# Entry of a two-layer diffusion backbone: the first two modulations' rows loaded two blocks per run into the activation places of two chunks

## The chip, the cores and the metric

The kernel runs as one program on one NeuronCore of a Trainium2 chip. The metric is the device time of one execution in microseconds (us), median over the runs; lower is better. All times below are from a profiled execution or from the timed runs of the kernel before the change.

## What is computed

The reference is a small diffusion backbone: 1024 latent tokens and 256 context tokens of width 1024, two layers. The first layer (even) mixes with four mLSTM heads beside 32 S5 state-space groups, the second (odd) with a gated DeltaNet; each layer also has a SwiGLU feed-forward part. What matters here stands at the very start. Every sub-layer normalises its rows and modulates them with a shift and a scale that come from a conditioning vector:

```python
s_lat = jax.nn.silu(c)
s_ctx = jax.nn.silu(c_ctx)
m_l = jnp.split((s_lat @ ada_w[i] + ada_b[i])[:, None, :], 6, axis=-1)
m_c = jnp.split((s_ctx @ ada_w[i] + ada_b[i])[None, None, :], 6, axis=-1)
hl = modulate(rmsnorm(x, norm1_w[i]), m_l[0], m_l[1])
hc = modulate(rmsnorm(ctx, norm1_w[i]), m_c[0], m_c[1])
```

`ada_w[i]` is 1024 x 6144 in float32; one modulation (shift or scale) needs a 1024 x 1024 block of it, 4 MB. Before the first projection of layer 0 can run, modulations 0 and 1 of layer 0 must be there, 8 MB of weights for two matrix-vector products each.

## The kernel before

Tokens are cut into three chunks: chunk 0 is the context (256 tokens), chunks 1 and 2 are 512 latent tokens each. A chunk is held transposed (features on the partitions) as `x0`, `x1`, `x2`. The normalised and modulated activations of a chunk are a pair of tiles `hh`/`hl` (a high and a low part, 128 x 8 x tokens, float32 bytes), allocated by `acts`; products run in three passes, high by high, low by high and high by low.

The function `entry` (line 1131) is the start of the program:

- `load_x` (line 329) loads the input in ten row blocks of 128 tokens x 1024 (512 KB each): two of the context, then eight latent ones, called x-block 0 to 7 below. Each lands in a tile `x_raw` of pool `araw`. ScalarE squares it and sums over the row (line 344; the squares themselves go to `junk`, a part of an activation tile), TensorE transposes it in eight pieces (line 349), VectorE and ScalarE copy the pieces into `x0` to `x2` (lines 352 and 354).
- `cond_steps` (line 182) makes one modulation. It loads `ada_w` in runs of `kk` row blocks (line 191), multiplies each block with the conditioning vector `svec` (line 194), copies the sum out of PSUM (`a_sb`, line 198), transposes it (`a_pt`, line 202) and adds the bias (`mod`, line 206); for the scale it also makes `amod` (line 210).
- `s5_poles` computes the poles of the S5 groups on VectorE, a chain of some 120 small instructions (lines 785 to 890); it needs only its own small inputs.
- `norm` makes the reciprocal root of a chunk's row sums (lines 223 and 94 to 102, VectorE) and a diagonal matrix of it (`ntmp`, line 231); TensorE spreads it over the partitions (`nb_ps`, line 275). `norm_part` then makes the eight feature blocks of `hh` and `hl` (lines 287, 289, 281 on VectorE, ScalarE, VectorE).
- `u_in` (S5 inputs) are the first projections of layer 0: they need `hh`/`hl` and the weights `w_raw` (line 113), which ScalarE rounds to `w_hi` (line 117) and GpSimd subtracts to `w_lo` (line 118).

Before the change `cond_many([(0, 0), (0, 1)], 1)` loads one row block (512 KB) per run, 16 runs. The tiles `a_raw` and `x_raw` share one tag of pool `araw` with three buffers, so a run of `ada_w` waits until the run or the x-block three loads earlier has been used. Every DMA of this stage is issued by SyncE (SP) in one order; a transfer also waits until the transfer eight issues earlier is complete, because the issues take eight semaphores in turn.

TensorE's instructions run in the order of the program text in this stage; on VectorE, ScalarE and SP the order is set by the framework's scheduler.

Of the kernel before, what the change touches and what calls it, by code (L numbers as in the profile page):

```python
# [6 lines left out]
F32 = mybir.dt.float32  # L7
# [9 lines left out]
P = 128  # L17
D = 1024
# [24 lines left out]
class Kernel:  # L43
# [135 lines left out]
        self.hnw = self.const.tile([P, 4], F32, name="hnw")  # L179
        nc.vector.tensor_scalar(out=self.hnw, in0=self.ncols[:, 32:36], scalar1=0.5, scalar2=None, op0=ALU.mult)  # L180

    def cond_steps(self, i, m, kk):


        nc = self.nc
        w = self.ins["ada_w"][i]
        ps = self.psm.tile([P, 512], F32, name="a_ps", tag="pm")
        for k0 in range(0, KB, kk):
            raw = self.araw.tile([P, kk, D], F32, name="a_raw", tag="a_raw")
            src = w[k0 * P:(k0 + kk) * P, m * D:(m + 1) * D]  # L190
            self.last_load = nc.sync.dma_start(out=raw, in_=src.rearrange("(k p) n -> p k n", p=P)).ins
            for k in range(k0, k0 + kk):
                for j in range(4):
                    nc.tensor.matmul(ps[32 * j:32 * j + 32, :256], self.svec[:, k], raw[:, k - k0, j * 256:(j + 1) * 256],
                                     start=(k == 0), stop=(k == KB - 1), tile_position=(0, 32 * j))
            yield
        sb = self.small.tile([P, 256], F32, name="a_sb", bufs=1)
        nc.vector.tensor_copy(sb, ps[:, :256])
        yield
        pt = self.psm.tile([P, 512], F32, name="a_pt", tag="pm")  # L200
        for h in range(2):
            nc.tensor.transpose(pt[:, h * P:(h + 1) * P], sb[:, h * P:(h + 1) * P], self.ident)
        src = pt[:, :256].rearrange("p (h j r) -> p j h r", h=2, r=32)[:, :, :, 0:2]
        dst = self.mod[:, i, m * 8:(m + 1) * 8].rearrange("p (j h) v -> p j h v", h=2)
        bias = self.adab[:, i, m * 8:(m + 1) * 8].rearrange("p (j h) -> p j h", h=2).unsqueeze(3)
        nc.vector.tensor_tensor(out=dst, in0=src, in1=bias.to_broadcast([P, 4, 2, 2]), op=ALU.add)
        if m in (1, 4):
            s = m // 4
            nw = self.ncols[:, 16 * s + 8 * i:16 * s + 8 * i + 8].unsqueeze(2).to_broadcast([P, 8, 2])
            nc.vector.scalar_tensor_tensor(out=self.amod[:, i, s], in0=self.mod[:, i, m * 8:(m + 1) * 8], scalar=1.0,  # L210
                                           in1=nw, op0=ALU.add, op1=ALU.mult)
        yield

    def cond_many(self, units, kk):
        for i, m in units:
            yield from self.cond_steps(i, m, kk)


    def norm_rstd(self, ssum_cols, n, scale=1.0 / D):
# [109 lines left out]
    def load_x(self, hs):  # L329

        nc = self.nc
        self.x = []
        self.ssq = self.const.tile([P, NCH], F32, name="ssq0")
        junk = hs[2][1].rearrange("p k t -> p (k t)")[:, :D]
        for ci, (t0, n) in enumerate(CHUNKS):
            xt = self.xp.tile([P, KB, n], F32, name=f"x{ci}")
            self.x.append(xt)
            src = self.ins["ctx"][0] if ci == 0 else self.ins["x"][0]
            r0 = 0 if ci == 0 else t0 - NCTX
            for j in range(n // P):  # L340
                raw = self.araw.tile([P, D], F32, name="x_raw", tag="a_raw")
                self.last_load = nc.sync.dma_start(out=raw, in_=src[r0 + j * P:r0 + (j + 1) * P, :]).ins
                ti = t0 // P + j
                nc.scalar.activation(out=junk, in_=raw, func=AF.Square, accum_out=self.ssq[:, ti:ti + 1])
                for h in range(2):
                    pt = self.psd.tile([P, 512], F32, name="x_pt", tag="pd")
                    for b in range(4):
                        f = h * 4 + b
                        nc.tensor.transpose(pt[:, b * P:(b + 1) * P], raw[:, f * P:(f + 1) * P], self.ident)
                    o = xt[:, h * 4:h * 4 + 4, j * P:(j + 1) * P]  # L350
                    if h == 0:
                        nc.vector.tensor_copy(o, pt.rearrange("p (b t) -> p b t", b=4))
                    else:
                        nc.scalar.copy(out=o, in_=pt.rearrange("p (b t) -> p b t", b=4))
                yield
# [372 lines left out]
    def emit(self, *streams):  # L728

        for _ in self.merge(streams):  # L730
            pass
# [399 lines left out]
    def entry(self, hs, mp, keep, st):  # L1131


        nc = self.nc
        norms = []

        def norm(ci):
            t0, n = CHUNKS[ci]
            rstd = self.norm_rstd(self.ssq[:, t0 // P:(t0 + n) // P], n // P)
            norms.append(self.norm_part(0, 0, ci, 0, n, hs[ci], rstd))  # L1140
            emit(norms[ci], 2)

        def emit(gen, n=1000):
            for _ in self.take(gen, n):
                pass

        x = self.load_x(hs)
        with ExitStack() as s1:
            cp = self.pool("cp", 1, st=s1)
            self.cond_vectors(cp)  # L1150
            poles = self.s5_poles(keep)
            next(poles)
            emit(x, 2)
            cond = self.cond_many([(0, 0), (0, 1)], 1)
            emit(cond, 2)
            emit(poles)
            emit(cond, 2)
            self.cond_columns(cp)
            emit(self.merge([(cond, 16), (self.take(x, 4), 4)]))
        u_in = self.s5_inputs(hs, mp, self.pool("wu", 1, st=st))  # L1160
        with self.tc.issue_after(self.last_load):
            emit(u_in, 1)
        norm(0)
        norm(1)
        emit(norms[0])
        emit(x, 2)
        emit(u_in, 3)
        emit(x)
        emit(norms[1])
        norm(2)  # L1170
        emit(u_in, 3)
        emit(norms[2])
        emit(u_in, 3)
        with self.tc.issue_after(self.last_load):
            for ci, (t0, n) in enumerate(CHUNKS):
                nc.sync.dma_start(out=self.x_dr[:, :, t0:t0 + n].rearrange("k p t -> p k t"), in_=self.x[ci])
        return u_in
# [214 lines left out]
    def layer0(self):  # L1392
# [6 lines left out]
        with ExitStack() as s0:  # L1399
            sk = ExitStack()  # L1400
            self.hy = self.hy2 = self.pool("hp", 1, st=s0)
            mp = self.pool("mp", 2, st=s0)
            gr = self.pool("mgr", 1, st=s0)
            self.s5k = self.pool("s5q", 1, st=sk)
            hs = [self.acts(ci) for ci in range(3)]
            with ExitStack() as s1:
                self.xp = self.pool("xp", 1, st=s1)
                self.araw = self.pool("araw", 3, st=s1)
                self.ntmp = self.pool("ntmp", 2, st=s1)
                order = ExitStack()  # L1410
                order.enter_context(self.in_pe_order())
                u_in = self.entry(hs, mp, mg, s1)
            self.even_select(mg)
            proj = self.mlstm_project(hs, mp)
            rows = self.mlstm_gate_rows(hs, gr)
            s5p = self.pool("s5s", 1, st=s5, other=True), self.pool("s5t", 2, st=s5, other=True)
            work = self.chain(u_in, rows, self.take(proj, NI))
            self.emit((self.take(work, W1), W1), (self.s5_inputs_outputs(), 5))
            self.emit((self.take(work, W2), W2))
            self.emit((work, 6 + NI - W1 - W2), (self.s5_in_matrices(), 16))  # L1420
            self.emit((self.take(proj, NJ), NJ))
            self.emit((self.take(proj, NP), NP), (self.s5_states(*s5p), 16))
            self.emit((self.take(proj, NK), NK))
            self.emit((self.take(proj, NQ), NQ), (self.s5_out_matrices(), 8))
            sk.close()
            self.emit((self.take(proj, NR), NR), (self.mlstm_gates(mg), 9))
            self.conv_taps()
            self.araw = self.pool("araw", 2, st=s0)
            self.emit((proj, 48 - NI - NJ - NK - NP - NQ - NR), (self.cond_many([(0, m) for m in range(2, 6)], 2), 24))
# [30 lines left out]
        places = ([wr.tile([P, KB * P], F32R, name=f"w_{p}") for p in ("hi", "lo")] for _ in range(KB // 2))  # L1460
# [939 lines left out]
```

## Time and profile before

| | |
|---|---|
| median of 3 timed runs | 3572.6 us (3568.52 to 3575.85) |
| the profiled execution's own time | 3570.8 us |
| its span, first to last instruction | 3568.8 us |
| mean granted TensorE clock | 0.967 |
| TensorE busy | 3341.3 us (94%) |
| VectorE busy | 1863.7 us (52%) |
| ScalarE busy | 1006.6 us (28%) |
| GpSimd busy | 971.9 us (27%) |

The page cuts the span in 40 slices of 89 us. In the first slice TensorE is busy for 5 tenths, its granted clock is 0.6 and the DMA engines are busy for 7 tenths; from the fourth slice on TensorE is nearly always at 9 or more. A busy TensorE is not one at its peak, since the ends of matmuls are modelled; idle time of an engine that nothing waits for costs nothing.

### The profile page before, as it was taken

To read this page: it belongs to the slowest core of one execution; us is meant where nothing else is said; L and a number is where in the kernel's file an instruction comes from. 1 tells how busy PE (TensorE), PEld (TensorE's weight loads), DVE (VectorE), ACT (ScalarE), POOL (GpSimd) and SP (SyncE) were. 2 spreads that over 40 slices of the span, in tenths; PEclk is the share of its full clock that TensorE was granted. 3 is DMA by queue.
4 is the path that set the end of the run, shared out by engine and by line. 5 is a ranking of instruction groups with operands and counts; after the bars stand their busy time and mean duration, and the time that the engine had idled before them with its cause. 6 is when DMAs were issued, how large, how long until landed. Compare 5 with 4: busy or idle time off the path is not lost. (4 is left out here: it accounts for less than half of the span.)

```text
span 3568.8 us, 48262 instructions
## 1 busy us (share of the span) xinstructions
PE 3341.3 (94%) x18518; PEld 2796.5 (78%) x18527; DVE 1863.7 (52%) x4024; ACT 1006.6 (28%) x2409; POOL 971.9 (27%) x843
## 2 busy tenths in 40 slices
PE   5998979899999999999988999888999999999999
PEld 3787768788888888888777877668897788888888
DVE  6749977624433333333467777776654432323234
ACT  3221125422111111111245545543444211111112
POOL 1011123241111111111342382753334122222223
PEclk6999989999999999999999999899999999999999
DMA  7454676331222121121123334356553011111111
GB/s 235 112 172 128 211 197 192 107 127 36 77 83 66 60 83 60 59 71 42 54 69 97 117 119 125 119 139 204 170 167 111 18 54 45 53 45 54 42 53 65
DMA packets 396187, 360.29 MB, mean 101 GB/s; under 512 B 104123, under 2 KB 329115, under 8 KB 395446
## 3 DMA queue, kind: packets, MB, share of 16 engines
q1 hardware_dynamic: 395958, 357.22, 32.4%
q8 instruction: 146, 2.39, 0.3%
q14 instruction: 83, 0.68, 0.1%
HBM read 258.92 MB, written 96.75 MB: 100 GB/s over the span
## 5 line engine op out<-in xcount | busy, mean ns | idle before, releaser
L124 PE MATMUL pd<-hh,w_hi 128*128 128x512 f32 (+1 forms) x3064 | 1158.2, 378 | 3.0 <-ACT hh L289 2.0
L126 PE MATMUL pd<-hh,w_lo 128*128 128x512 f32 (+1 forms) x3064 | 1134.6, 371 | 5.6 <-POOL w_lo L118 5.2
L125 PE MATMUL pd<-hl,w_hi 128*128 128x512 f32 (+1 forms) x3064 | 1137.5, 371 | 2.4 <-DVE hl L281 2.2
L118 POOL TENSOR_TENSOR w_lo<-w_raw,w_hi 128x1024 fp32r<-128x1024 f32 (+2 forms) x205 | 479.8, 2341 | 2001.5 <-ACT w_hi L117 1977.3
L124 PEld LDWEIGHTS pd<-hh,w_hi 128*128 128x128 f32 x3064 | 587.1, 192 | 118.4 <-issue 6.0
L126 PEld LDWEIGHTS pd<-hh,w_lo 128*128 128x128 f32 x3064 | 585.8, 191 | 111.4 <-POOL w_lo L118 9.3
L125 PEld LDWEIGHTS pd<-hl,w_hi 128*128 128x128 f32 x3064 | 586.8, 192 | 102.4 <-DVE hl L281 5.3
L117 ACT CAST w_hi<-w_raw 128x1024 fp32r<-128x1024 f32 (+2 forms) x205 | 207.4, 1012 | 927.1 <-PE pd L125 695.2
L1344 DVE SCALAR_TENSOR_TENSOR x<-pd,mod,x 128x512 f32<-128x512 f32 (+1 forms) x408 | 265.6, 669 | 226.1 <-PE pd L126 226.1
L124 PE MATMUL pd<-g_hi,w_hi 128*128 128x512 f32 (+1 forms) x844 | 307.8, 365 | 0.0
L125 PE MATMUL pd<-g_lo,w_hi 128*128 128x512 f32 (+1 forms) x844 | 306.9, 364 | 0.0
L126 PE MATMUL pd<-g_hi,w_lo 128*128 128x512 f32 (+1 forms) x844 | 304.1, 363 | 0.6 <-POOL w_lo L118 0.6
L1703 DVE SCALAR_TENSOR_TENSOR cv_acc<-img,wcv,cv_acc 128x512 f32<-128x512 f32 x384 | 279.6, 751 | 40.0 <-ACT img L1674 24.9
L1332 DVE TENSOR_TENSOR ntmp<-ntmp,pd 128x512 f32<-128x512 f32 (+1 forms) x110 | 69.8, 634 | 416.0 <-PE pd L126 415.6
L1331 DVE SCALAR_TENSOR_TENSOR ntmp<-ntmp,pd 128x512 f32<-128x512 f32 (+1 forms) x110 | 69.7, 634 | 380.8 <-ACT ntmp L1330 380.8
L124 PEld LDWEIGHTS pd<-g_hi,w_hi 128*128 128x128 f32 x844 | 159.2, 189 | 27.9 <-ACT w_hi L117 2.5
L126 PEld LDWEIGHTS pd<-g_hi,w_lo 128*128 128x128 f32 x844 | 158.9, 188 | 26.4 <-POOL w_lo L118 1.0
L125 PEld LDWEIGHTS pd<-g_lo,w_hi 128*128 128x128 f32 x844 | 159.2, 189 | 24.5
L1334 DVE SCALAR_TENSOR_TENSOR g_lo<-ntmp,g_hi 128x512 fp32r<-128x512 f32 (+1 forms) x110 | 139.8, 1270 | 64.1 <-ACT g_hi L1333 64.1
L1333 ACT ACTIVATE g_hi<-ntmp 128x512 fp32r<-128x512 f32 (+1 forms) x110 | 64.7, 588 | 349.2 <-DVE ntmp L1332 348.9
L1330 ACT ACTIVATE ntmp<-pd 128x512 f32<-128x512 f32 (+1 forms) x110 | 60.7, 552 | 247.9 <-PE pd L126 247.9
L250 POOL TENSOR_TENSOR nacc<-nacc,ntmp 128x256 f32<-128x256 f32 (+1 forms) x72 | 74.2, 1035 | 125.5 <-ACT ntmp L246 124.0
(544 smaller groups left out, 4531.4 us busy)
## 6 DMA issues: line engine op xcount, KB each, us to landing
w_raw<-in_ffn_w_dram SPq DMA_DIRECT2D x106, 512.0 KB
a_raw<-in_ada_w_dram SPq DMA_DIRECT2D x40, 1024.0 KB
w_raw<-in_od_w_in_dram SPq DMA_DIRECT2D x32, 512.0 KB
w_raw<-in_ffn_w_dram SPq DMA_DIRECT2D x32, 384.0 KB
w_raw<-in_ev_w_in_dram SPq DMA_DIRECT2D x20, 512.0 KB
a_raw<-in_ada_w_dram SPq DMA_DIRECT2D x16, 512.0 KB
x_dr<-x SPq DMA_DIRECT2D x4, 2048.0 KB
p_dr<-mp_t SPq DMA_DIRECT2D x32, 256.0 KB
```

The lines of the kernel that those rows point to most:

```text
L117: nc.scalar.copy(out=hi, in_=raw)
L118: self.w_lo_engine.tensor_tensor(out=lo, in0=raw, in1=hi.bitcast(F32), op=ALU.subtract)
L124: mm(ps, lh, rh, start=first, stop=False)
L125: mm(ps, lh, rl, start=False, stop=False)
L126: mm(ps, ll, rh, start=False, stop=last)
L250: nc.gpsimd.tensor_tensor(out=acc, in0=acc, in1=sq, op=ALU.add)
L1331: nc.vector.scalar_tensor_tensor(out=th[:, :n], in0=th[:, :n], scalar=1.0, in1=p1, op0=ALU.add, op1=ALU.mult)
L1332: nc.vector.tensor_tensor(out=th[:, :n], in0=th[:, :n], in1=p3, op=ALU.mult)
L1333: nc.scalar.activation(out=gh[:, t0:t0 + n], in_=th[:, :n], func=AF.Copy, scale=0.5)
L1334: nc.vector.scalar_tensor_tensor(out=gl[:, t0:t0 + n], in0=th[:, :n], scalar=0.5, in1=gh[:, t0:t0 + n].bitcast(F32), op0=ALU.mult, op1=ALU ...
L1344: nc.vector.scalar_tensor_tensor(out=xd, in0=ps, scalar=g, in1=xd, op0=ALU.mult, op1=ALU.add)
L1703: nc.vector.scalar_tensor_tensor(out=a, in0=src, scalar=wc(i), in1=a, op0=ALU.mult, op1=ALU.add)
```

## The change

- `cond_steps` and `cond_many` take an iterator `places`. With it a run of `ada_w` lands in a place given from outside, not in a buffer of `araw`.
- `entry` allocates the activation pairs of chunks 1 and 2 (`hh1`, `hl1`, `hh2`, `hl2`, each 16 KB on a partition), cuts each in two, and loads all eight runs of two row blocks (1 MB each) there. Nothing waits for a buffer among these loads. They are called run 0 to 7 below.
- `araw` keeps its three buffers, now for the input blocks alone.
- The interleaving is written anew: run 0, the poles, `cond_columns`, then five steps of the modulations (runs 1 to 3, the copy and the transpose of modulation 0), then runs of modulation 1 with x-blocks 0 to 3 between.
- `hs` holds only chunk 0 at first; the pairs of chunks 1 and 2 are allocated a second time, in the same places, after the modulations. `junk` moves from chunk 2's `hl` to chunk 0's for the context and chunk 1, since chunk 2's holds weights by then.

```diff
-    def cond_steps(self, i, m, kk):
+    def cond_steps(self, i, m, kk, places=None):
...
-            raw = self.araw.tile([P, kk, D], F32, name="a_raw", tag="a_raw")
+            raw = next(places) if places else self.araw.tile([P, kk, D], F32, name="a_raw", tag="a_raw")
...
-        junk = hs[2][1].rearrange("p k t -> p (k t)")[:, :D]
         for ci, (t0, n) in enumerate(CHUNKS):
...
+            junk = hs[2 if ci == 2 else 0][1].rearrange("p k t -> p (k t)")[:, :D]
...
             emit(x, 2)
-            cond = self.cond_many([(0, 0), (0, 1)], 1)
-            emit(cond, 2)
+
+            flat = [h.bitcast(F32).rearrange("p k t -> p (k t)") for ci in (1, 2) for h in self.acts(ci)]
+            places = iter([f[:, o:o + 2 * D].rearrange("p (k n) -> p k n", n=D) for f in flat for o in (0, 2 * D)])
+            cond = self.cond_many([(0, 0), (0, 1)], 2, places)
+            emit(cond, 1)
             emit(poles)
-            emit(cond, 2)
             self.cond_columns(cp)
-            emit(self.merge([(cond, 16), (self.take(x, 4), 4)]))
+            emit(cond, 5)
+            emit(self.merge([(cond, 6), (self.take(x, 4), 4)]))
         u_in = self.s5_inputs(hs, mp, self.pool("wu", 1, st=st))
         with self.tc.issue_after(self.last_load):
             emit(u_in, 1)
+        hs.extend(self.acts(ci) for ci in (1, 2))
...
-            hs = [self.acts(ci) for ci in range(3)]
+            hs = [self.acts(0)]
```

On SP before, from the last small load of `cond_columns` to the last of the four x-blocks that chunk 1 needs (`a_raw` is a run of `ada_w`, `x_raw` an x-block, `g_bias` four tiny loads for the mLSTM gates):

```order
L174 DMA n_rows<-in_od_head_norm_w_dram 8x128
L191 DMA a_raw<-in_ada_w_dram 128x1024
L434 DMA g_bias<-in_ev_i_bias_dram 4x1 x2
L434 DMA g_bias<-in_ev_f_bias_dram 4x1
...
L191 DMA a_raw<-in_ada_w_dram 128x1024 x3
L342 DMA x_raw<-in_x_dram 128x1024
L191 DMA a_raw<-in_ada_w_dram 128x1024 x2
L342 DMA x_raw<-in_x_dram 128x1024
L191 DMA a_raw<-in_ada_w_dram 128x1024 x4
L342 DMA x_raw<-in_x_dram 128x1024
L191 DMA a_raw<-in_ada_w_dram 128x1024 x4
L342 DMA x_raw<-in_x_dram 128x1024
```

On SP now, the same stretch, with what each issue waits for (DMAHW0 to 7 are the eight semaphores; the wait is for the transfer eight issues earlier. PE and Activation are the readers of an `x_raw` buffer):

```order
L174 DMA n_rows_369<-in_od_head_norm_w_dram 8x128 [waits DMAHW6_49]
L191 DMA hh1_195<-in_ada_w_dram 128x2x1024 [waits DMAHW7_49]
L191 DMA hl1_196<-in_ada_w_dram 128x2x1024 [waits DMAHW0_49]
L191 DMA hl1_196<-in_ada_w_dram 128x2x1024 [waits DMAHW1_49]
L191 DMA hh2_197<-in_ada_w_dram 128x2x1024 [waits DMAHW2_49]
L342 DMA x_raw_425<-in_x_dram 128x1024 [waits DMAHW3_49]
L191 DMA hh2_197<-in_ada_w_dram 128x2x1024 [waits DMAHW4_49]
L342 DMA x_raw_449<-in_x_dram 128x1024 [waits DMAHW5_49,PE_49,Activation_49]
L191 DMA hl2_198<-in_ada_w_dram 128x2x1024 [waits DMAHW6_49]
L191 DMA hl2_198<-in_ada_w_dram 128x2x1024 [waits DMAHW7_49]
L342 DMA x_raw_482<-in_x_dram 128x1024 [waits DMAHW0_49,PE_49,Activation_49]
...
L342 DMA x_raw_499<-in_x_dram 128x1024 [waits DMAHW5_49,PE_49,Activation_49]
```

The waits for the products of earlier runs are gone; between x-block 2 and x-block 3 stand the four `g_bias` loads (left out here).

On TensorE before, from the biases to the first spread of a norm:

```order
L194 MATMUL a_ps<-a_raw,svec 32x256 x8
L349 MATMUL x_pt<-ident,x_raw 128x128 x8
L194 MATMUL a_ps<-a_raw,svec 32x256 x8
L202 MATMUL a_pt<-ident,a_sb 128x128 x2
L349 MATMUL x_pt<-ident,x_raw 128x128 x8
L194 MATMUL a_ps<-a_raw,svec 32x256 x16
L349 MATMUL x_pt<-ident,x_raw 128x128 x8
L194 MATMUL a_ps<-a_raw,svec 32x256 x16
L349 MATMUL x_pt<-ident,x_raw 128x128 x8
L202 MATMUL a_pt<-ident,a_sb 128x128 x2
```

On TensorE now, the same stretch (eight rows of line 194 are one run of 1 MB):

```order
L194 MATMUL a_ps<-hh_195,svec 32x256 x8
L194 MATMUL a_ps<-hl_196,svec 32x256 x16
L202 MATMUL a_pt<-ident,a_sb 128x128 x2
L194 MATMUL a_ps<-hh_197,svec 32x256 x8
L349 MATMUL x_pt<-ident,x_raw 128x128 x8
L194 MATMUL a_ps<-hh_197,svec 32x256 x8
L349 MATMUL x_pt<-ident,x_raw 128x128 x8
L194 MATMUL a_ps<-hl_198,svec 32x256 x16
L349 MATMUL x_pt<-ident,x_raw 128x128 x16
L202 MATMUL a_pt<-ident,a_sb 128x128 x2
```

Modulation 0 is finished ahead of the first x-block, x-blocks 2 and 3 stand together at the end. Behind the entry the order on TensorE is the same; on the other engines a few neighbours change places.

## Rows read from the trace of the kernel before

**Rows 1.** Busy time by stage (columns: window: length, PE, PEld, DVE, ACT, POOL busy, PEclk, DMA share, GB/s).

```profile
12.00:52.00 40.00, 23.02 (x155) 9.53 (x156) 21.07 (x132) 6.17 (x11) 0.00 (x0) 0.57 0.81 264
52.00:60.00 8.00, 2.31 (x9) 1.58 (x7) 7.44 (x17) 3.89 (x7) 4.67 (x2) 0.71 0.84 283
60.00:92.00 32.00, 23.54 (x112) 19.48 (x113) 24.86 (x51) 16.66 (x31) 2.39 (x1) 0.71 0.66 210
92.00:140.00 48.00, 48.00 (x229) 39.88 (x229) 28.28 (x44) 10.36 (x17) 2.68 (x3) 0.99 0.57 96
```

**Rows 2.** TensorE's waits from 10 to 51 us (waited for: total us, times, longest).

```profile
PE a_ps L194 <- DMA a_raw<-in_ada_w_dram: 13.4, 11, 2.6
PE x_pt L349 <- DMA x_raw<-in_x_dram: 1.8, 3, 0.8
```

**Rows 3.** Four shorter windows of the entry, columns as in group 1.

```profile
4.00:8.00 4.00, 1.83 (x9) 1.76 (x10) 1.49 (x5) 1.65 (x4) 3.04 (x15) 1.00 0.96 353
14.00:17.00 3.00, 0.35 (x5) 0.20 (x8) 2.30 (x16) 0.00 (x0) 0.00 (x0) 0.51 0.97 355
28.00:31.00 3.00, 1.64 (x10) 1.02 (x7) 1.43 (x8) 0.75 (x1) 0.00 (x0) 0.50 1.00 388
44.00:48.00 4.00, 2.37 (x20) 0.60 (x24) 0.65 (x4) 0.00 (x0) 0.00 (x0) 0.50 0.80 271
```

**Rows 4.** Timeline of SP's DMA issues (start, length, engine, line, operation, count).

```profile
7.68 0.27 SPq L174 DMA_DIRECT2D n_rows<-in_od_head_norm_w_dram  x1
9.43 0.35 SPq L191 DMA_DIRECT2D a_raw<-in_ada_w_dram  x1
...
45.41 0.33 SPq L342 DMA_DIRECT2D x_raw<-in_x_dram  x1
...
47.38 6.04 SPq L342 DMA_DIRECT2D x_raw<-in_x_dram  x3
```

**Rows 5.** Timeline of TensorE (start, length, instructions; in brackets the idle time before).

```profile
10.03 0.91 PE L194 MATMUL a_ps<-a_raw,svec 128*32 128x256 f32 x8
13.21 0.64 PE L194 MATMUL a_ps<-a_raw,svec 128*32 128x256 f32 x8 [2.27 <-DMA a_raw<-in_ada_w_dram]
...
18.03 1.08 PE L194 MATMUL a_ps<-a_raw,svec 128*32 128x256 f32 x8 [0.21 <-DMA a_raw<-in_ada_w_dram]
...
51.09 1.94 PE L349 MATMUL x_pt<-ident,x_raw 128*128 128x128 f32 x8 [2.21 <-DMA x_raw<-in_x_dram]
52.82 0.63 PE L202 MATMUL a_pt<-ident,a_sb 128*128 128x128 f32 x2
...
74.06 0.41 PE L125 MATMUL pd<-hl,w_hi 128*128 128x256 f32 x1
...
79.06 0.28 PE L125 MATMUL pd<-hl,w_hi 128*128 128x256 f32 x1
...
89.67 1.42 PE L124 MATMUL pd<-hh,w_hi 128*128 128x512 f32 x1
```

**Rows 6.** Timeline of VectorE (as group 5).

```profile
14.12 0.26 DVE L789 COPY s_lam<-s_pt 128x96 f32<-128x96 f32 x1 [1.64 <-PE s_pt L787]
...
53.49 0.17 DVE L206 TENSOR_TENSOR mod<-a_pt,adab 128x16 f32<-128x16 f32 x1
...
53.70 2.28 DVE L210 SCALAR_TENSOR_TENSOR amod<-mod,ncols 128x16 f32<-128x16 f32 x1
...
56.08 2.19 DVE L100 TENSOR_TENSOR rs_a<-ny 128x4 f32<-128x4 f32 x1
```

**Rows 7.** DMA issues from 0 to 130 us (queue, count, KB each).

```profile
a_raw<-in_ada_w_dram SPq DMA_DIRECT2D x16, 512.0 KB
x_raw<-in_x_dram SPq DMA_DIRECT2D x8, 512.0 KB
```

**Rows 8.** VectorE alone over the chain of the poles (length, DVE busy, PEclk, DMA share, GB/s).

```profile
14.10:44.70 30.60, 20.19 (x129) 0.56 0.78 264
```

**Rows 9.** Timeline of GpSimd from 40 to 100 us (as group 5).

```profile
53.59 4.67 POOL L118 TENSOR_TENSOR w_lo<-w_raw,w_hi 128x1024 fp32r<-128x1024 f32 x2 [41.80 <-ACT w_hi L117]
```

More of the change, by code (lines that the diff above doesn't have):

```diff
@@ L212, in cond_steps, with cond_many @@
         yield
-    def cond_many(self, units, kk):
+    def cond_many(self, units, kk, places=None):
         for i, m in units:
-            yield from self.cond_steps(i, m, kk)
+            yield from self.cond_steps(i, m, kk, places)
     def norm_rstd(self, ssum_cols, n, scale=1.0 / D):
```

## The prediction

> **What bounds the kernel now.** I read the time by stage first. From 92 us on TensorE is busy without a gap (48.00 of 48) and at full clock; before that it is not: 23.02 of 40 us at a clock of 0.57 between 12 and 52, then 2.31 of 8 and 23.54 of 32 while VectorE, with 7.44 of 8 and 24.86 of 32, is the busiest [rows 1]. So the entry has two parts: one up to 52 us, in which nothing is saturated, and one up to 92 us that VectorE paces. The change touches the first. There TensorE's waits say what ends last: 13.4 us for runs of `ada_w`, 1.8 us for x-blocks, nothing of weight for an engine [rows 2]. Next, whether the DMA engines could do more: over 12 to 52 us they carry 264 GB/s at a share of 0.81 [rows 1], and where their share is 0.96 to 1.00 they carry 353 to 388 [rows 3]. So loads are late because they are issued late, by the three shared buffers. The last x-block of chunk 1 (x-block 3) is issued at 45.41 and transposed at 51.09; the transpose of modulation 1 follows at 52.82 [rows 4, 5], `mod` at 53.49 [rows 6]. That is the point that the change can bring forward; all behind it hangs on it.
>
> **The change part by part.**
>
> *Bytes and issue.* Up to x-block 3 nothing is saved: behind run 0 come seven runs of 1024 KB and four x-blocks of 512 KB (sizes by [rows 7]), 9216 KB or 9.44 MB. Run 0 doubles: with the two context blocks 2.10 MB stand ahead of run 1, of which 353 GB/s bring 1.41 by 8 us [rows 3]; the other 0.69 at 0.37 MB/us end at 9.9, and with some 0.6 us until the semaphore SP issues run 1 at about 10.5. It must wait for that, since run 0 stands eight issues earlier; before, the second run went out at 9.43 [rows 4]. The DMA engines drain meanwhile: an estimated loss of 1.1 us. A lone run issued at 9.43 was multiplied at 13.21 [rows 4, 5], 3.8 us, of which 0.52 MB at 0.37 are 1.4; so 2.4 us pass ahead of the stream.
>
> *The stream.* From there up to eight transfers stand in the queue. Each issue waits for the one eight earlier, which leaves run 6, run 7 and x-block 2 ahead of x-block 3 when it is issued, some 7 us of transfer, so I expect no further hole. The rate is the unknown. Lower bound 0.30 MB/us: above the 271 GB/s of 44 to 48 us, where loads still waited for buffers [rows 3], since that wait goes. Upper bound 0.40, just above the best window, 388 [rows 3]. I take 0.37, between the windows at a share near 1. Then x-block 3 lands at 10.5 + 2.4 + 9.44/0.37 = 38.4 us, against 51.09: 12.7 us earlier.
>
> The Trainium skill ("DMA: Bandwidth & Descriptors", Specifications) gives about 358 GB/s as the HBM limit per core, below what I take. By it the stream would last an estimated 26.4 us in place of 25.5, and x-block 3 land 0.9 us later. The window with 388 [rows 3] speaks against it as a limit for one core alone.
>
> *TensorE at the tail.* In this stretch it runs at a granted clock of 0.5 [rows 3], the lower of its two levels (1.2 GHz), where 512 KB of products take 1.08 us and an x-block's transposes 1.94 [rows 5]. Run 7 lands 2.8 us before x-block 3, at 35.6; its products end at 37.8, x-block 2's transposes at 39.7, x-block 3's at 41.6. There `a_pt` of modulation 1 starts, against 52.82: **11.2 us earlier**. The tail eats 1.5 of the 12.7. At the upper clock (a run of 512 KB in 0.64 [rows 5]) it would be nearly free.
>
> *VectorE.* The poles start when TensorE has transposed their input, behind run 0's products: at about 12, not 14.12 [rows 6]. The chain with its copies is 20.2 us of work [rows 8], so 32.2, and perhaps 4 us of waits for run 3's sum and the x-blocks between: 36, under 41.6. Hidden by some 5 us; without that cover it would be the next bound.
>
> *Buffers, junk, double allocation.* The first write to chunk 1's `hh` must wait for products that ended long before; the squares into chunk 0's `hl` precede that chunk's own parts on ScalarE. Nothing. The `g_bias` loads move behind x-block 2 and are read only later: nothing, as long as the 7 us stand ahead of x-block 3.
>
> *From 52 to 92 us.* Same work in nearly the same order. The two 2.2 us stretches on VectorE (`amod` and one `rs_a`, at 53.70 and 56.08), tiny instructions, lie beside GpSimd's two `w_lo` from 53.59 on [rows 6, 9]; weights and modulation move together, so these stay. X-block 4 is issued at 47.38 before, 3.7 us ahead of x-block 3's landing [rows 4, 5], now about 1.4 ahead, because it waits for x-block 2; its transposes stand behind both spreads of the norms, which wait for VectorE: covered. TensorE's clock may fall at other places: at the low level a 256-column product took 0.41, at the high one 0.28 [rows 5], and some 30 of them met the low one, at 0.1 us each. That is up to 3 us either way.
>
> *Behind 92 us.* TensorE has no gap there, SP's and VectorE's work hangs on it or on the entry, and no transfer is near the DMA's limit (96 GB/s [rows 1]): the shift passes on. In layer 1 a few neighbours change places on VectorE, ScalarE and GpSimd; I put 2 us either way on that.
>
> *Sum.* 3570.8 - 11.2 = 3559.6 for an execution like the profiled one, which lies 1.8 under the median of the runs: **3561 us**. Bounds of the rate: at 0.30, x-block 3 lands at 44.4, run 7 at 40.9, `a_pt` starts at 46.9, a gain of 5.9; at 0.40, landing 36.5, `a_pt` 39.8, a gain of 13, or up to 15 with the clock up.
>
> **The rivals.** A measurement of this kernel can tell about 0.2%, 7.1 us, from no change.
>
> *The stream is no faster than 0.30.* For it: over the whole stretch the DMA carried 264 GB/s at a share of 0.81 [rows 1], which scaled to a full share is 326, not 370. Against: three windows at 353 to 388 [rows 3]. Gain 5 to 6: 3567 us.
>
> *The gain is given back before 92 us.* VectorE is already full there [rows 1], x-blocks 5 to 7 now wait for each other's buffers and semaphores, and TensorE may meet the low clock in all of chunk 0's first products (about 96 of them, 9 us in place of 3). Each x-block that comes later relative to its norm costs its delay. Gain 2 to 5: 3569 us.
>
> *Slower: the queued transfers share the engines in place of following each other.* Before, at most three loads were under way, and they arrived one behind the other: one run was multiplied 1.3 us after its predecessor (idle only 0.21 us at 18.03 [rows 5]). Now run 1 to 6 and two x-blocks, 7.3 MB, are under way together. If they shared, all would arrive near 31 us; TensorE, in program order, would then do six runs (13.0), four x-blocks (7.8) and run 7 (2.2) in a row: 54 us, and the poles, which stand behind `a_sb` of modulation 0 on VectorE, would end near 53. `mod` would come 1 to 2 us later than at 53.49, with a stream of 0.30 some 7 us later: 3574 to 3580. It decides from the point at which run 1 arrives less than a microsecond before run 4.
>
> The Trainium skill ("DMA: Bandwidth & Descriptors", Queues, rings and completion order) says both that each DMA engine takes its descriptors in ring order and that completion need not be first in, first out. By the first this rival falls away, and the arrivals above agree with it; no run here shows a deep queue.
>
> **How the numbers follow.** Forecast (gain 8 to 15) 0.70; slow stream 0.17; given back 0.08; shared 0.05. Faster by over 0.2%: 0.67 from the forecast and 0.06 from the slow stream, 0.73. Within 0.2%: 0.03, 0.11, 0.08 and 0.02, 0.24. Slower: 0.03. The range runs from 3552 (gain 15, plus 3 from the clock, plus 3 that the runs differ among themselves) to 3568 (the slow stream and part of the second rival); about 2 in 10 lie outside.
>
> **What would show it.** Right: runs of 1 MB multiplied 2.5 to 3.2 us apart, the DMA share above 0.95 from 13 to 38 us, TensorE's wait for `ada_w` at 5 us or less, x-block 3 transposed by 42, `mod` at 42 to 43, chunk 1's 512-column products beginning at 78 to 79, not at 89.67 [rows 5], and the same distance from there to the end. Wrong: holes in the stream beyond the one near 10 us, VectorE's poles ending behind x-block 3, runs arriving in a bunch, or a start of chunk 1's products that is not earlier by what `mod` gained.

## The result, and the profile after

| | before | after |
|---|---|---|
| median of the timed runs | 3572.6 us (3566.49 to 3575.85, 5 runs) | 3554.2 us (3548.97 to 3556.28, 5 runs) |
| profiled execution, own time | 3570.8 us | 3549.0 us |
| its span | 3568.8 us | 3547.2 us |
| mean granted TensorE clock | 0.967 | 0.973 |

The changed kernel takes 0.995 of the time before (95% interval 0.9938 to 0.9963). The medians differ by 18.4 us. The forecast was 3561 us, a gain of 11.6, so the direction and the place are right, and the size is more than a third too small.

First the stages of the changed kernel (columns as in [rows 1]). They answer to [rows 1, 3]:

```profile
10.00:12.00 2.00, 1.48 (x14) 0.69 (x16) 1.69 (x11) 0.59 (x1) 1.85 (x8) 1.00 0.31 48
12.00:16.00 4.00, 1.25 (x12) 0.47 (x4) 3.59 (x25) 0.00 (x0) 0.00 (x0) 0.95 0.90 332
16.00:38.00 22.00, 15.77 (x139) 7.29 (x140) 17.34 (x108) 4.71 (x9) 0.00 (x0) 0.70 1.03 396
40.00:52.00 12.00, 5.17 (x27) 4.00 (x27) 10.91 (x24) 7.83 (x14) 4.94 (x3) 0.72 0.66 200
52.00:80.00 28.00, 21.37 (x105) 17.76 (x104) 25.01 (x49) 14.44 (x26) 2.10 (x1) 0.82 0.66 220
```

The DMA engines carry 396 GB/s at a share of 1.03 over 22 us, where they had carried 264 at 0.81 over 40 us [rows 1]. The only hole is the one near 10 us. From 40 us on VectorE is the busiest engine, as before.

TensorE's waits from 10 to 40 us, against the 13.4 and 1.8 us of [rows 2]:

```profile
PE a_ps L194 <- DMA hl<-in_ada_w_dram: 4.5, 4, 1.5
PE a_ps L194 <- DMA hh<-in_ada_w_dram: 3.7, 2, 3.1
PE x_pt L349 <- DMA x_raw<-in_x_dram: 0.7, 3, 0.3
PE a_pt L202 <- DVE a_sb L198: 0.5, 1, 0.5
```

TensorE's timeline (columns as in [rows 5]):

```profile
16.48 1.93 PE L194 MATMUL a_ps<-hh,svec 128*32 128x256 f32 x16 [3.13 <-DMA hh<-in_ada_w_dram]
...
35.30 1.07 PE L194 MATMUL a_ps<-hl,svec 128*32 128x256 f32 x16 [1.49 <-DMA hl<-in_ada_w_dram]
...
37.96 1.06 PE L349 MATMUL x_pt<-ident,x_raw 128*128 128x128 f32 x8 [0.21 <-DMA x_raw<-in_x_dram]
38.86 0.38 PE L202 MATMUL a_pt<-ident,a_sb 128*128 128x128 f32 x2
...
46.83 2.08 PE L275 MATMUL nb_ps<-ntmp,ones 128*128 128x512 f32 x2 [7.15 <-DVE ntmp L231]
...
72.56 1.12 PE L275 MATMUL nb_ps<-ntmp,ones 128*128 128x512 f32 x2 [3.44 <-DVE ntmp L231]
73.12 0.95 PE L124 MATMUL pd<-hh,w_hi 128*128 128x512 f32 x1
```

Run 1 is multiplied at 16.48 and run 7 at 35.30, each behind a wait for its own transfer; x-block 3 follows at 37.96 instead of 51.09, `a_pt` of modulation 1 at 38.86 instead of 52.82 [rows 5], and chunk 1's 512-column products at 73.12 instead of 89.67.

VectorE's timeline answers to [rows 6], GpSimd's to [rows 9]:

```profile
37.11 0.18 DVE L878 COPY s_ai<-s_npi 128x32 f32<-128x32 f32 x1
...
40.24 0.17 DVE L206 TENSOR_TENSOR mod<-a_pt,adab 128x16 f32<-128x16 f32 x1
...
40.76 2.21 DVE L100 TENSOR_TENSOR rs_a<-ny 128x4 f32<-128x4 f32 x1
43.00 2.26 DVE L101 SCALAR_TENSOR_TENSOR rs_a<-rs_a,nv 128x4 f32<-128x4 f32 x1
```

```profile
40.56 4.68 POOL L118 TENSOR_TENSOR w_lo<-w_raw,w_hi 128x1024 fp32r<-128x1024 f32 x2 [28.64 <-ACT w_hi L117]
```

The poles end at 37.1, less than 2 us ahead of `a_pt`. The two 2.2 us stretches moved along with the weights: they again lie beside GpSimd's two `w_lo`.

One execution is not enough to place the gain, so both kernels were traced twice (the second time in the last experiments below):

| start (on TensorE, but for the first row), us | before | before, again | after | after, again | gain of the means |
|---|---|---|---|---|---|
| squares of x-block 3 (on ScalarE) | 51.03 | 50.92 | 37.91 | 37.68 | 13.2 |
| `a_pt` of modulation 1 | 52.82 | 52.71 | 38.86 | 39.88 | 13.4 |
| spread `nb_ps` of chunk 1 | 60.04 | 60.03 | 46.83 | 46.96 | 13.1 |
| chunk 1's 512-column products | 89.67 | 88.36 | 73.12 | 74.74 | 15.1 |
| first transpose of the output | 3526.86 | 3527.03 | 3505.27 | 3512.26 | 18.2 |

So 13 us are won up to `a_pt` and chunk 1's spread, 2 more up to chunk 1's products, and 3 appear somewhere in the 3430 us behind. The experiments take these three parts in turn.

### The profile page after: what moved, and what is told of

It reads as the page before. It is cut to its first block, busy times and chain, and to the rows that moved or that the text cites. A ratio compares the mean times of both kernels' runs of the same rounds, so it can differ in the third digit from the quotient of the medians.

```text
span 3547.2 us, 48237 instructions
## 1 busy us (share of the span) xinstructions
PE 3325.0 (94%) x18518; PEld 2788.2 (79%) x18527; DVE 1864.3 (53%) x4024; ACT 1005.8 (28%) x2409; POOL 966.6 (27%) x843
```

## Experiments

### The order alone, and the places alone

Two kernels split the change. `e1_order` keeps the shared buffers and 512 KB runs and takes only the new interleaving:

```diff
-            emit(cond, 2)
             self.cond_columns(cp)
-            emit(self.merge([(cond, 16), (self.take(x, 4), 4)]))
+            emit(cond, 8)
+            emit(self.merge([(cond, 10), (self.take(x, 4), 4)]))
```

> The kernel before with the new order of the modulations alone (modulation 0 finished first, then modulation 1 between x-blocks 0 to 3), still 512 KB per run in the three shared buffers. If the gain comes from the places (theory): SP still waits for the products of earlier runs, the DMA share between 12 and 48 us stays near 0.8, x-block 3 is transposed at 49 to 52 us and the time is within 4 us of before, about 3572. If the order made the gain (rival): x-block 3 at 38 to 42 us and about 3556.

Measured: 3570.1 us, ratio 1.0 (0.9991 to 1.0009). The stream is as before, with x-block 3 at 50.52:

```profile
12.00:52.00 40.00, 23.02 (x157) 9.37 (x158) 21.68 (x135) 6.37 (x11) 0.00 (x0) 0.58 0.83 266
```

`e2_places` takes the other half, the changed kernel with runs of one block, each in a place of its own (the line that cuts the places is left out here), and the order of before:

```diff
...
-            cond = self.cond_many([(0, 0), (0, 1)], 2, places)
-            emit(cond, 1)
+            cond = self.cond_many([(0, 0), (0, 1)], 1, places)
+            emit(cond, 2)
             emit(poles)
+            emit(cond, 2)
             self.cond_columns(cp)
-            emit(cond, 5)
-            emit(self.merge([(cond, 6), (self.take(x, 4), 4)]))
+            emit(self.merge([(cond, 16), (self.take(x, 4), 4)]))
```

> The new places alone: 512 KB per run as before, emitted in the order of before, each of the 16 runs in a place of its own. If the places make the gain (theory): DMA share near 1.0 from 13 us on, x-block 3 transposed at 37 to 40 us, the time within 4 us of the changed kernel, about 3555. If the order of the modulations or the 1 MB run is what counts (rivals): x-block 3 at 44 to 51 us, 3564 to 3573.

Measured: 3557.0 us, ratio 0.9963 (0.9949 to 0.9977). x-block 3 is transposed at 37.80 and `a_pt` starts at 38.70:

```profile
10.00:13.00 3.00, 2.27 (x27) 0.61 (x25) 2.69 (x15) 0.59 (x1) 1.75 (x8) 1.00 0.93 361
13.00:38.00 25.00, 17.13 (x135) 7.33 (x136) 20.04 (x129) 5.47 (x10) 0.00 (x0) 0.73 0.96 361
```

The places make the gain and the order does not (the median is 2.8 us above the change's, and the intervals overlap). With the places the x-blocks also have the three buffers to themselves; the two were not separated. There is no hole at 10 us here, yet the stream ends no earlier; its hole is only later (165 GB/s from 12 to 16 us).

### The length of a run

```diff
...
-            cond = self.cond_many([(0, 0), (0, 1)], 2, places)
-            emit(cond, 1)
+            cond = self.cond_many([(0, 0), (0, 1)], 1, places)
+            emit(cond, 2)
             emit(poles)
             self.cond_columns(cp)
-            emit(cond, 5)
-            emit(self.merge([(cond, 6), (self.take(x, 4), 4)]))
+            emit(cond, 8)
+            emit(self.merge([(cond, 10), (self.take(x, 4), 4)]))
```

(The places are cut to one block as in `e2_places`.)

> The changed kernel with one row block per run (16 runs of 512 KB) in the same places and nearly the same order. If the length of a run does not count (theory): the first wait for a semaphore ends earlier (run 0 is half as long), x-block 3 transposed at 36 to 38.5 us, the time within 3 us of the changed kernel. If 1 MB runs are what fills the DMA engines (rival): share below 0.95 and x-block 3 at 41 us or later, 3 us or more slower than the changed kernel.

Measured: 3551.7 us, ratio 0.9946 (0.9931 to 0.9961), inside the change's interval. x-block 3 is at 37.95 (37.96 with 1 MB), with 104 GB/s from 10 to 13 us and 389 from 13 to 38. Runs of 512 KB stream as fast as runs of 1 MB; the length is not part of the gain.

### GpSimd's subtraction beside VectorE

```diff
         with self.tc.issue_after(self.last_load):
+        self.w_lo_engine = nc.vector
             emit(u_in, 1)
+        self.w_lo_engine = nc.gpsimd
```

(The two lines stand around the `with` block; the first three `w_lo` of the entry run on VectorE.)

> The changed kernel with the low parts of the first three S5 input weights made on VectorE in place of GpSimd. If the 2.2 us stretches of tiny VectorE instructions come from GpSimd's subtraction beside them (theory): these become 0.2 us each, VectorE pays some 1.2 us per weight itself, the diagonal of chunk 1's norm is made 1.5 to 2.5 us earlier than at 46.1 and the time falls by 1 to 3 us against the changed kernel. If the stretches have another cause (rival): they stay, VectorE pays the 3.6 us on top, and the diagonal is 2 us later.

Measured: 3555.0 us, ratio 0.9951 (0.9935 to 0.9967). VectorE's timeline at the place of the two stretches:

```profile
40.18 1.22 DVE L118 TENSOR_TENSOR w_lo<-w_raw,w_hi 128x1024 fp32r<-128x1024 f32 x1
...
41.50 0.16 DVE L100 TENSOR_TENSOR rs_a<-ny 128x4 f32<-128x4 f32 x1
...
43.70 0.69 DVE L231 TENSOR_TENSOR ntmp<-ident,ny 128x512 f32<-128x512 f32 x1
```

With GpSimd idle the same tiny instructions take 0.16 us, and `ntmp` stands at 43.70 instead of 46.08, although VectorE now does the subtractions itself. That shows the cause: they were held for as long as GpSimd's `w_lo` ran. The Trainium skill ("SBUF — State Buffer", SBUF: two separate sides) says that a VectorE instruction with two SBUF inputs and a GpSimd instruction that reads SBUF take one pair of ports in turn, each for its whole length. The trace agrees: the instructions held are such ones, for 2.2 us, about the length of one `w_lo` (4.68 for two).

The 1 to 3 us that were expected in the total time are not seen: 2 us are won at chunk 1 (`nb_ps` at 44.45 instead of 46.83) and are within the spread of the rest.

### Filling the hole: moved, then removed

`e6_early_issue` issues run 1 directly behind run 0, ahead of the small loads of `cond_columns`:

```diff
...
             emit(cond, 1)
+            raw1 = next(places)
+            nc.sync.dma_start(out=raw1, in_=self.ins["ada_w"][0][2 * P:4 * P, 0:D].rearrange("(k p) n -> p k n", p=P))
+            self.early[1] = raw1
             emit(poles)
```

(The part left out makes `cond_steps` use this place and not load run 1 again.)

> Run 1 is issued right behind run 0, ahead of the small loads; the place, the length and the order of the products stay as in the change. Theory A (the stream of loads sets the end of the entry's first part, and the hole near 10 us, 48 GB/s at a share of 0.31 from 10 to 12 us, is part of its price): no window of 2 us from 8 to 36 us is under 300 GB/s, x-block 3 is transposed at 36.7 to 37.2 instead of 37.96 and a_pt of modulation 1 starts at 37.6 to 38.1 instead of 38.86; 0.8 to 1.2 us less in time, too little to tell by the runs. Theory B (VectorE is the next bound: its poles end at 37 in the change, only 1 us ahead of x-block 3): the loads come earlier but a_pt does not by more than 0.4 us, and TensorE waits there for a_sb or for a copy by VectorE. Theory C (the small loads that now stand behind 1 MB more come late, and with them s5_lam and the poles): lam after 12.78 by over 1 us and the poles' end after 38.

Measured: 3552.3 us, ratio 0.9946 (0.9931 to 0.9961); x-block 3 at 37.95. All three theories missed the reason. SP's last small load and run 2, and two windows (from 10 to 12 us it is 375 GB/s now):

```profile
10.85 0.27 SPq L174 DMA_DIRECT2D n_rows<-in_od_head_norm_w_dram  x1
13.43 0.90 SPq L194 DMA_DIRECT2D hl<-in_ada_w_dram  x2
```

```profile
12.00:14.00 2.00, 0.56 (x6) 0.30 (x3) 1.46 (x11) 0.00 (x0) 0.00 (x0) 1.00 0.45 162
14.00:16.00 2.00, 1.41 (x18) 0.63 (x18) 1.65 (x12) 0.00 (x0) 0.00 (x0) 1.00 0.78 156
```

Run 2 now stands eight issues behind run 1, with the seven small loads between, and waits for run 1's landing. The hole is as large and 2 us later. `e9_no_hole` spreads the small loads, two or three behind each of runs 1 to 3, and moves their transposes behind modulation 0's sum:

```diff
...
+            if places and k0:
+                for out, in_ in self.small_loads[:2 if k0 < KB - kk else 3]:
+                    nc.sync.dma_start(out=out, in_=in_)
+                del self.small_loads[:2 if k0 < KB - kk else 3]
...
-            self.cond_columns(cp)
-            emit(cond, 5)
+            emit(cond, 4)
+            emit(columns)
+            emit(cond, 1)
```

> The seven small loads of the bias and norm columns no longer stand together between run 0 and run 1; two or three follow each of run 1, run 2 and run 3, and their transposes and copies stand behind modulation 0's sum. Theory A (an issue waits for the one eight earlier; a crowd of small loads in those eight leaves the engines one large transfer, so the hole only moved in e6_early_issue; spread out, it goes): no window of 2 us from 8 to 36 us under 300 GB/s, and the stream ends 2 us earlier, x-block 3 transposed at 35.5 to 36.5 instead of 37.96. Theory B (not only the hole but the engines' total sets the end, near 9.4 MB in 28 us whatever the order, as three kernels with holes at different places landed x-block 3 at 37.8 to 38.0): x-block 3 again at 37.5 to 38. On a_pt: VectorE's poles end near 37, so that a_pt comes at 37.3 to 38 under theory A, mod at 38.7 to 39.5 instead of 40.24, and nb_ps of chunk 1 up to 1.5 us earlier; if VectorE's slack is larger than I think, a_pt at 36.5 to 37.2. Time: 0 to 1.5 us under the change's own.

Measured: 3552.4 us, ratio 0.9947 (0.9931 to 0.9962). The hole is gone:

```profile
12.00:14.00 2.00, 1.64 (x17) 0.59 (x13) 0.99 (x6) 0.00 (x0) 0.00 (x0) 1.00 1.05 391
16.00:36.00 20.00, 13.66 (x122) 6.92 (x123) 17.46 (x113) 4.85 (x9) 0.00 (x0) 0.73 1.04 398
```

TensorE at the end of the stream, and chunk 1's spread:

```profile
33.13 1.93 PE L197 MATMUL a_ps<-hl,svec 128*32 128x256 f32 x16 [1.49 <-DMA hl<-in_ada_w_dram]
34.99 3.68 PE L352 MATMUL x_pt<-ident,x_raw 128*128 128x128 f32 x16
38.46 0.57 PE L205 MATMUL a_pt<-ident,a_sb 128*128 128x128 f32 x2
...
45.44 2.08 PE L278 MATMUL nb_ps<-ntmp,ones 128*128 128x512 f32 x2 [5.97 <-DVE ntmp L234]
```

Run 7 is multiplied 2.17 us earlier, so the hole cost 2.2 us. But `a_pt` gains only 0.4, and stands at 38.46 and not at the 37.3 to 38 that were expected: in this execution the granted clock is 0.50 from 34 to 38 us, and run 7's products and the two x-blocks take 5.6 us in a row instead of the 3.2 of the change. The tail of TensorE, which the prediction had feared, is real, at the lower clock. `mod` is even 0.67 us later than in the change (40.91 against 40.24), because VectorE makes it behind an instruction of the norm that stands for 2.33 us beside GpSimd's `w_lo`; and yet chunk 1's `nb_ps` comes 1.39 us earlier, at 45.44. It follows the row sums of x-block 3, which reach VectorE 2.19 us earlier (36.90 against 39.09), and not the modulation.

### The x-blocks last

```diff
-            emit(self.merge([(cond, 6), (self.take(x, 4), 4)]))
+            emit(self.merge([(cond, 4), (self.take(x, 2), 2)]))
+            emit(cond)
+            emit(x, 2)
```

> The last two x-blocks of chunk 1 are loaded and transposed behind run 7 and behind the modulation, in place of ahead of the modulation. Theory A (what the modulation hangs on is the last transfer ahead of it, whatever it is): run 7 lands two x-blocks, some 2.6 us, earlier, at about 32.7 instead of 35.3, its products end at 33.8. If VectorE were free, a_pt would start near 34.5. Theory B (VectorE's poles, which end at 36.8 to 37.1, are the next bound): a_sb waits for them, a_pt starts at 36.5 to 37.5, mod comes at 37.5 to 38.5 instead of 40.24. In both, the first norm of chunk 1 still needs x-block 3, whose transposes stay at 38 or come later, so that nb_ps of chunk 1 (46.83 in the change) comes earlier by 0 to 2 us, and the time falls by 0 to 2 us, within the spread of the runs.

Measured: 3557.7 us, ratio 0.9959 (0.9946 to 0.9973).

```profile
35.01 1.07 PE L194 MATMUL a_ps<-hl,svec 128*32 128x256 f32 x16 [1.40 <-DMA hl<-in_ada_w_dram]
36.83 0.44 PE L202 MATMUL a_pt<-ident,a_sb 128*128 128x128 f32 x2 [0.75 <-DVE a_sb L198]
...
46.67 1.22 PE L275 MATMUL nb_ps<-ntmp,ones 128*128 128x512 f32 x1 [7.23 <-DVE ntmp L231]
```

Run 7 comes only 0.29 us earlier, not 2.6: x-blocks 2 and 3 stand behind run 7 in the stream of the change already, as the prediction has it and this expectation had not. So neither theory was tried as it was meant. Without their transposes ahead of it, `a_pt` waits 0.75 us for `a_sb` on VectorE; 0.55 of that is what `a_pt` of modulation 0 waits too, with VectorE idle ahead of its copy, so the poles hold it by some 0.2 us. `mod` is 2.9 us earlier, at 37.30, and chunk 1's `nb_ps` only by 0.16: chunk 1 hangs on the x-blocks and the norm's tiny instructions, not on the modulation.

### Two edits together

`e7_early_and_vector` is `e6_early_issue` with the `w_lo` of `e5_lo_vector`; `e10_no_hole_and_vector` is `e9_no_hole` with them.

> Run 1 issued early as in e6_early_issue, and the low halves of the first input weight subtracted on VectorE as in e5_lo_vector. Theory A (each is on the path that sets the end, at its own place): nb_ps of chunk 1 comes at 43.4 to 44 instead of 46.83, chunk 2's at 70 to 71 instead of 72.56, and the time is 2 to 3.5 us under the change's own, 3549 to 3553 for the median. Theory B (what is won ahead of 92 us is lost again behind it when VectorE's order moves, as in e5_lo_vector, whose 2 us at 92 us were gone at the end): no gain over the change, 3553 to 3557.

Measured: 3554.9 us, ratio 0.9954 (0.994 to 0.9968); `nb_ps` at 44.75, later than theory A has it, chunk 1's products at 71.55.

> e9_no_hole and the low halves on VectorE together. Theory A (two places on the path, gains add): nb_ps of chunk 1 at 43 to 44 instead of 46.83, chunk 2's at 70 to 71 instead of 72.56, the shift at 92 us 18.5 to 20.5 us against the kernel before, the median 3549 to 3553. Theory B (behind 92 us the rest of the program differs by some us from one order and one execution to the next, which hides it): the same shift at 92 us, the median 3553 to 3556.

Measured: 3552.7 us, ratio 0.9949 (0.9937 to 0.9962); `a_pt` at 37.36, `nb_ps` at 42.57, chunk 1's products at 70.06, 3 to 4.7 us ahead of the change's two traces. The edits add up at their place (at `nb_ps` 4.3 us, against 1.4 and 2.4 alone). The medians do not tell either version from the change, so none of these is shown to be faster than it.

### Both kernels once more

> The change itself once more, for a second trace and more times: the spread of what is gained behind 92 us. Theory A (the 17 us at 92 us are the gain, and the step to 21 near 1730 to 1800 us is one execution's own): the shift against the profile of the kernel before is again 16 to 18 at 92 us, and differs from 21 at the end by over 1 us. Theory B (the step belongs to the kernel's order downstream): the same jumps at the same places, 19 from 560 and 21 to 22 from 1795 on.

> The kernel before once more, for a second trace. Theory A (the gain behind 92 us is one execution against another): TensorE's matmuls stand 1 to 4 us apart from those of the first trace of before somewhere behind 92 us, with steps at the places where the change's traces have them (500 to 670, 1780 to 2360 us). Theory B (the steps belong to the change): the two traces of before run within 0.5 us of each other.

Measured: 3553.8 us for the change (4 runs, ratio 0.9951, 0.9937 to 0.9964; 16.3 below the median of before in the same set, where the first set has 18.4), 3571.0 for the kernel before (one run). Matmul by matmul, the second trace of before runs between 2.7 us behind the first and 5.6 ahead of it (2.5 behind from 360 to 400 us, 0.6 ahead at 452, 2.75 ahead from 670 to 1795, 5.6 at 2499) and is even with it again from 2788 on. The two traces of the change are 1.6 us apart at chunk 1's products and 7.0 at the output. Against the first trace of before, the second of the change is 15.0 us ahead at 100 us, less than the 16 to 18 that were expected, and 14.6 at the end, without the step to 21. So the steps behind 92 us belong to single executions, as theory A has it for both kernels.

From chunk 1's first product to the first output transpose it is 3437.2 and 3438.7 us in the traces of before, 3432.2 and 3437.5 in those of the change, and 3434.3 to 3442.5, 3438.1 on the mean, in the eight experiments that have the places. As far as these traces tell, the program behind 92 us is as long as it was, and two executions of one kernel differ there by some 5 us (those of the change).

## Why the prediction was right, and where its terms were off

**The bound and the mechanism hold.** Loads were late because they were issued late, by the buffers: the places alone give the gain, the order alone none. None of the three rivals came: the stream was faster than 0.30 MB/us, nothing was given back before 92 us, and the runs did not share the engines but were multiplied one behind the other, 2.5 to 3.9 us apart (the longer distances with an x-block between). Three of the signs that were set for "right" missed their numbers. TensorE waited 8.2 us for `ada_w`, not 5 or less: 3.1 at the hole, and 1.4 and 1.5 ahead of runs 6 and 7, since at the upper clock each was done some 0.9 us sooner (1.07 for 1.93). `mod` came at 40.24 and not at 42 to 43, chunk 1's products at 73.12 and not at 78 to 79; the parts below say why.

**The stream: two errors that cancelled.** x-block 3 was put at 38.4 and stood at 37.96. The hole was sized at 1.1 us and cost 2.2, by `e9_no_hole`; the rate was taken as 0.37 MB/us and was 0.396, close to the upper bound of 0.40. The 9.44 MB then take 23.8 us, not 25.5, behind a start of 14.1, not 12.9. The prediction drew the rate from windows at a DMA share of 0.96 to 1.00 [rows 3]; in the changed kernel the share was 1.03. That the landing came out within 0.5 us is luck. The Trainium skill's figure of 358 GB/s per core, which the prediction weighed ("DMA: Bandwidth & Descriptors", Specifications), does not bound this kernel on its one core: here 396 GB/s were held for 22 us. The Trainium skill ("HBM Reference", Specifications (TRN2)) says about 425 for a core that streams alone, and the trace fits under it.

**TensorE's tail: mis-sized, and not what chunk 1 hung on.** The prediction went as far as `mod`, since "all behind it hangs on it", and let the tail eat 1.5 of the 12.7 us ahead of it. The runs show x-block 3 itself in that place. ScalarE sums its squares, VectorE makes the norm's diagonal of them, and for that TensorE waits. Before:

```profile
51.03 1.06 ACT L344 ACTIVATE hl<-x_raw 128x1024 fp32r<-128x1024 f32 x1 [8.71 <-DMA x_raw<-in_x_dram]
52.22 0.17 DVE L223 TENSOR_SCALAR nv<-ssq 128x4 f32<-128x4 f32 x1 [2.85 <-ACT hl L344]
59.30 0.69 DVE L231 TENSOR_TENSOR ntmp<-ident,ny 128x512 f32<-128x512 f32 x1
```

And in the changed kernel, ahead of the `nb_ps` at 46.83 shown above:

```profile
37.91 1.06 ACT L344 ACTIVATE hl<-x_raw 128x1024 fp32r<-128x1024 f32 x1
39.09 0.17 DVE L223 TENSOR_SCALAR nv<-ssq 128x4 f32<-128x4 f32 x1 [1.05 <-ACT hl L344]
46.08 0.69 DVE L231 TENSOR_TENSOR ntmp<-ident,ny 128x512 f32<-128x512 f32 x1
```

Each of them stands 13.1 to 13.2 us earlier, as x-block 3's transposes do. `nb_ps` does not follow the modulation: with `mod` 2.9 us earlier it gains 0.16 (`e8_blocks_last`), with `mod` 0.67 later it comes 1.39 earlier (`e9_no_hole`), and in the second trace of the change, with `a_pt` 1.0 later, it is 0.13 later. So the gain that passes on is that of x-block 3, put at 12.7, and the 1.5 should not have come off. A slow tail can cost something by another way: in `e9_no_hole` VectorE waits 0.58 us for the transposes of an x-block, between the row sums and the norm's next step. What a tail as late as the forecast one (`a_pt` at 41.6) would have done was not tried.

Its size was off too. The prediction took the granted clock of 0.50 that it had there before [rows 3]. In the changed trace the clock was 0.50 from 16 to 28 us and 1.00 from 30 to 42; TensorE had been busy for 3.60 of the 4 us from 24 to 28, with the transpose of modulation 0, run 4 and x-block 0 in a row. So a run took 1.07 instead of the 2.16 that were put and an x-block 1.06 instead of 1.94, and `a_pt` stood 0.9 us behind x-block 3's first transpose, not 3.2: 2.3 us of the 2.7 by which `a_pt` came earlier than forecast (38.86 against 41.6). The second trace has the low clock for part of the tail and `a_pt` at 39.88, `e9_no_hole` has it for all of it. A bound at each clock was right; taking the low one as the value was not. Why the clock rose there in one execution and not in another stays open.

**VectorE's cover was 1 to 2 us, not 5.** The poles ended at 37.1, 1 us later than put, and `a_pt` came 2.7 us earlier. In `e8_blocks_last`, with `a_pt` 2 us earlier still, the poles held `a_sb` by some 0.2 us.

**From 52 to 92 us: 1.4 of 2 us that were to be read from the order.** The prediction said "Same work in nearly the same order" and left only the clock. VectorE copies its part of x-blocks 6 and 7 out of PSUM as soon as TensorE has transposed them. Between the first of its two copies and chunk 2's diagonal `ntmp`, for which TensorE waits, stood six steps of chunk 1's features before:

```profile
82.46 0.69 DVE L352 COPY x<-x_pt 128x512 f32<-128x512 f32 x1 [0.75 <-PE x_pt L349]
83.06 0.74 DVE L281 SCALAR_TENSOR_TENSOR hl<-ntmp,mod,hh 128x512 fp32r<-128x512 f32 x1
83.72 0.68 DVE L352 COPY x<-x_pt 128x512 f32<-128x512 f32 x1
84.32 0.74 DVE L281 SCALAR_TENSOR_TENSOR hl<-ntmp,mod,hh 128x512 fp32r<-128x512 f32 x1
84.98 1.40 DVE L287 SCALAR_TENSOR_TENSOR ntmp<-x,amod,nb_ps 128x512 f32<-128x512 f32 x2
86.52 1.41 DVE L281 SCALAR_TENSOR_TENSOR hl<-ntmp,mod,hh 128x512 fp32r<-128x512 f32 x2
87.85 0.68 DVE L231 TENSOR_TENSOR ntmp<-ident,ny 128x512 f32<-128x512 f32 x1
```

And in the changed kernel four:

```profile
67.85 0.69 DVE L352 COPY x<-x_pt 128x512 f32<-128x512 f32 x1 [1.07 <-PE x_pt L349]
68.45 0.74 DVE L287 SCALAR_TENSOR_TENSOR ntmp<-x,amod,nb_ps 128x512 f32<-128x512 f32 x1
69.11 0.74 DVE L281 SCALAR_TENSOR_TENSOR hl<-ntmp,mod,hh 128x512 fp32r<-128x512 f32 x1
69.77 0.68 DVE L352 COPY x<-x_pt 128x512 f32<-128x512 f32 x1
70.37 0.74 DVE L287 SCALAR_TENSOR_TENSOR ntmp<-x,amod,nb_ps 128x512 f32<-128x512 f32 x1
71.03 0.75 DVE L281 SCALAR_TENSOR_TENSOR hl<-ntmp,mod,hh 128x512 fp32r<-128x512 f32 x1
71.81 0.69 DVE L231 TENSOR_TENSOR ntmp<-ident,ny 128x512 f32<-128x512 f32 x1
```

From the first copy to the diagonal it is 5.39 us before and 3.96 now, two steps of some 0.7 us less: one is done ahead of the copy, where VectorE waits for TensorE, and one behind the diagonal. TensorE's wait for the diagonal falls by as much, from 4.86 to 3.44, and both traces of each kernel agree on these four numbers. `e1_order` has the old wait, all kernels with the places 3.44 or less, so it comes with the places, not with the new interleaving. Why the scheduler puts them so was not tried. Of the other 0.6 us, some 0.35 are the clock, inside the 3 us that were left for it (from this spread to chunk 1's products it was 1.09 in both traces of before, 0.56 and 0.91 now); the rest is within what the traces of one kernel differ by.

**Behind 92 us.** The shift passes on, as put, though not for the reason given: "TensorE has no gap there" was read from 92 to 140 us [rows 1], and from 92 us to the end TensorE was busy for 3288 of 3476 us before. The 3 us that the last line of the table adds to the 15.1 are of the size by which two executions of one kernel differ there, and the mean over eight other kernels adds none; the 18.4 and 16.3 of the medians are some 15 by cause, and what the rest is stays open.

**The sum by what the runs show:** 13.1 up to chunk 1's spread, by x-block 3 (12.7 less 1.5 put), 1.4 by VectorE's order (0 put), 0.6 by the clock and by chance: together 15.1 on the mean (16.6 and 13.6 in the two pairs of traces). The forecast of the size fell short by the tail that was taken off and by the order that was not read.

## What to carry to other kernels

When loads wait for buffers, give them room that is idle at that time; here the order and the size of the transfers mattered less. Then count the issues between two large transfers: a group of small loads that fills the window of outstanding issues drains the engines, and issuing the large one earlier only moves the hole. Before a tail is costed, ask whether what comes next waits for it at all, and cost it at both levels of the clock; and compare the new order on the busiest engine at each place where another waits for it, not only where the edit is.

## What the runs showed of the hardware that was not expected

- One core held 389 to 398 GB/s from HBM for 20 to 25 us, with transfers of 512 KB and of 1 MB alike, at a DMA share of 1.02 to 1.04.
- Moving three subtractions of 128 x 1024 from GpSimd (2.3 us each) to VectorE (1.22 us each) made VectorE itself faster at that place, since its tiny instructions (0.16 us) no longer stood for 2.2 us each beside GpSimd's.
- The granted clock at one and the same place differs between executions of one kernel: two x-blocks' transposes took 2.1 us of work from 36.7 us on in one trace of the change and 3.60 from 36.5 on in the other.
